# Strassen products in three of eight weight quads of a feed-forward's input pairs, on one core

## The chip, the cores and the metric

One core of a Trainium2 chip runs the whole program once. The metric is device time in microseconds (us), the median of three runs. The matrix engine is TensorE (PE); its products land in PSUM, eight banks of 512 float32 columns per partition. VectorE (DVE) and ScalarE (ACT) work element by element, SyncE (SP) issues the loads.

## The reference

A transformer layer of width 2048 for 256 tokens, in float32: a feed-forward, a mixer, a second feed-forward, a final norm.

```python
def swiglu(h, w_in, w_out):
    a, b = jnp.split(h @ w_in, 2, axis=-1)
    return (jax.nn.silu(a) * b) @ w_out
...
        x = x + 0.5 * swiglu(rmsnorm(x, ffn1_norm[l]), ffn1_w_in[l], ffn1_w_out[l])
        x = x + hybrid_mixer(rmsnorm(x, mix_norm[l]), ...)
        x = x + 0.5 * swiglu(rmsnorm(x, ffn2_norm[l]), ffn2_w_in[l], ffn2_w_out[l])
```

`w_in` is 2048 x 11264 (two halves of 5632 columns, for `a` and `b`), `w_out` 5632 x 2048. The mixer is one projection of 2048 x 13312, three branches (convolution, pooling, attention) with output products and gates, and a last product of 2048 x 2048. All that this change rewrites in substance is `h @ w_in` of the two feed-forwards.

## The kernel before, in words

Tokens lie in two tiles of 128. Every large product is cut into chunks of 512 output columns, each chunk into groups of four k-tiles of 128 rows. A group is one load of 1 MB (`raw`, 128 partitions x 4 x 512), from `emit_dma` (L106) on SP's queue, three buffers deep. To keep float32 accuracy on the faster product type, both operands are split into a high part, a rounded copy, and a low part, the rest. `emit_split` does that for half a group at a time: ACT copies 1024 columns (`whi`, L119), DVE subtracts (`wlo`, L120). `emit_mm` (L133) then issues three products for each k-tile and token tile: high x high, high x low, low x high; a product reads 512 columns and adds into a PSUM accumulator of two banks (`acc`, two buffers; `side` for transposes and the like, two buffers).

The order of the program is written out by the loop at the end (from L569): for each group and half group it issues the load three groups ahead, the split three half groups ahead, one pending side step (`pop_side`: transposes and small products that follow an evacuation by a few half groups), and the products. Each engine runs its own instructions in that order.

A feed-forward (`ffn`, L207) has eleven pairs of chunks. The pair's first chunk (`a`) is evacuated through ACT's sigmoid (L219) and a DVE product (L221), the second (`b`) multiplies into the same tile (L229); eight transposes (L174) turn the gated tile, and it is split into `gh`, `gl` (L157, L158). After six pairs, and again after the other five, four output chunks are multiplied and added to the residual `xr` (L244).

At the start the loads go out in quarters. The first two chunks take turns, so that x is needed more slowly; x comes in four quarters (`x0raw`), each scaled by the norm's gain and split on ACT (L165) and DVE (L166).

Of the kernel before, what the change touches and what calls it, by code (L numbers as in the profile page):

```python
# [26 lines left out]
FF_HALVES = (6, 5)  # L27
KH = 2
WHOLE = ((0, KH),)
HALVES = tuple((k, k + 1) for k in range(KH))  # L30
UNITS = 29
RAW_BUFS = 3
SPLIT_BUFS = 5
LOOK_DMA = 3
LOOK_SPLIT = 3
# [3 lines left out]
SQ = 13  # L39
# [18 lines left out]
def hybrid_trunk(ctx: ExitStack, tc: tile.TileContext, x, xT, wst, vecs, poolw, fnorm, consts, out):  # L58
# [4 lines left out]
    up = ctx.enter_context(tc.tile_pool(name="up", bufs=UNITS))  # L63
    wp = ctx.enter_context(tc.tile_pool(name="wp", bufs=RAW_BUFS))
    sp = ctx.enter_context(tc.tile_pool(name="sp", bufs=2))
    psA = ctx.enter_context(tc.tile_pool(name="psA", bufs=2, space=bass.MemoryType.PSUM))
    psB = ctx.enter_context(tc.tile_pool(name="psB", bufs=2, space=bass.MemoryType.PSUM))
# [4 lines left out]
    dist = cp.tile([P, P + S], F32, name="dist")  # L72
    pw = {}

    def unit(name, dt, shape=(P, KG, S)):
        """A tile of 4 KiB per partition; all of them share one set of buffers."""
        return up.tile(list(shape), dt, tag="unit", name=name)
# [6 lines left out]

    def side_psum():
        return psB.tile([P, KG, S], F32, tag="side", name="side")

    groups = []
# [3 lines left out]
    def chunk(lhs, nk, evac, tail=False):  # L92
        """One 512-column chunk of a product: lhs(i) gives the split transposed operand of k-group i."""
        ch = {}
        for i in range(nk):
            groups.append(dict(lhs=lhs, i=i, first=i == 0, last=i == nk - 1, evac=evac, tail=tail, chunk=ch))

    raw_t, split_t = {}, {}

    def emit_dma(n, cuts=1):  # L100
        if n >= len(groups):
            return
# [4 lines left out]

    def emit_split(m, parts=WHOLE):
        n, half = divmod(m, KG // KH)
        if n >= len(groups):  # L110
            return
        r = raw_t[n]
        if m not in split_t:
            split_t[m] = (wp.tile([P, KH, CH], F32R, tag="hi", name="whi", bufs=SPLIT_BUFS),
                          wp.tile([P, KH, CH], F32R, tag="lo", name="wlo", bufs=SPLIT_BUFS))
        h, l = split_t[m]
        for k0, k1 in parts:
            rv = r[:, half * KH + k0:half * KH + k1]
            nc.scalar.activation(h[:, k0:k1], rv, AF.Copy)  # L119
            nc.vector.tensor_sub(l[:, k0:k1], rv, f32(h[:, k0:k1]))  # L120

    def emit_mm(m, tt, acc, cols=slice(0, CH)):
        n, half = divmod(m, KG // KH)
        g = groups[n]
        h, l = split_t[m]
        ah, al = g["lhs"](g["i"])
        for k in range(KH):
            ka = half * KH + k
            todo = [(i, t, a, b) for t in tt for i, a, b in ((0, ah, h), (1, ah, l), (2, al, h))]
            if n == 0:  # L130
                todo.sort(key=lambda e: (0, 2, 1)[e[0]])
            for i, t, a, b in todo:
                nc.tensor.matmul(acc[t], a[:, ka, t * P:(t + 1) * P], b[:, k, cols],  # L133
                                 start=g["first"] and ka == 0 and i == 0,
                                 stop=g["last"] and ka == KG - 1 and i == 2)
# [3 lines left out]
    def later(*steps):  # L139
        """PE work that follows an evacuation: one step at a time, some half groups after it."""  # L140
        for i, f in enumerate(steps):
            urgent.append((now[0] + DELAY + i * GAP, f))
# [27 lines left out]
    def transpose8(src, ps):  # L170
        """src(t, k): [128 tokens, 128 channels]; ps[channel, k, token]."""
        for k in range(KG):
            for t in range(NT):
                nc.tensor.transpose(ps[:, k, t * P:(t + 1) * P], src(t, k), idn)  # L174
# [394 lines left out]
    for n in range(len(groups)):  # L569
# [11 lines left out]
        if n in (0, 2):  # L581
            load_xT(n // 2 + 2)
# [170 lines left out]
```

## Time and profile before

| | |
|---|---|
| median of three runs | 2297.21 us (2296.74 to 2297.72) |
| profiled execution, first to last instruction | 2295.9 us |
| PE busy | 2285.1 us |
| DVE busy | 1207.4 us |
| ACT busy | 1015.2 us |
| granted PE clock, mean | 0.999 |
| loads, mean over the span | 191 GB/s |

The median is 1.3 us above the profiled execution's span. Busy time of PE is modelled at the ends of its pipelined products, so a busy PE says only that it did not wait; the price of a product is read from long unbroken stretches. Idle time of DVE and ACT costs nothing as long as PE is not waiting for them.

### The profile page before, as it was taken

The numbers are of one execution on the slowest core, as the hardware profiler recorded it, in microseconds if no ns is written. First come the engines' busy times: TensorE is split into PE (matmuls) and PEld (weight loads), VectorE is DVE, ScalarE is ACT, GpSimd is POOL, SyncE is SP. The second block draws the span as 40 slices with busy tenths as digits, with TensorE's granted clock in tenths as the row PEclk, the third lists the DMA queues.
The fourth block names the chain that finished last, engine by engine and source line by source line (L and its number), as shares of the span: only waits on it lengthen the run. The fifth ranks groups of instructions, "written<-read, shape, count | busy, mean of one in ns | idle before, by whom it ended". The sixth has DMA issues, their size and how long they took to land.

```text
span 2295.9 us, 25201 instructions
## 1 busy us (share of the span) xinstructions
PE 2285.1 (100%) x10349; PEld 1895.8 (83%) x10349; DVE 1207.4 (53%) x1206; ACT 1015.2 (44%) x1140; POOL 3.7 (0%) x9
## 2 busy tenths in 40 slices
PE   9999999999999999999999999999999999999998
PEld 7888888888888888888888888888888888888887
DVE  6554544545555565544554554555554544545554
ACT  6444433434445444445554444354444433444443
POOL 0000000000000000000000000000000000000000
PEclk9999999999999999999999999999999999999999
DMA  8545555555445545454545555445555455545454
GB/s 317 186 189 193 186 185 205 194 183 197 177 179 216 194 166 202 181 192 172 188 165 184 207 196 184 183 184 186 199 181 204 183 183 203 199 185 185 183 201 147
DMA packets 63476, 438.68 MB, mean 191 GB/s; under 512 B 7168, under 2 KB 7936, under 8 KB 11264
## 3 DMA queue, kind: packets, MB, share of 16 engines
q1 hardware_dynamic: 63360, 437.06, 51.8%
q8 instruction: 81, 1.33, 0.2%
q14 instruction: 35, 0.29, 0.0%
HBM read 434.94 MB, written 2.10 MB: 190 GB/s over the span
## 4 chain that ended last, share of the span: by engine, by line
PE 99%; DMA 0%; SPq 0%; DVE 0%; issue 0%; POOLq 0%; ACT 0%; DVEq 0%
PE acc L133 94%; PE side L133 2%; PE side L174 2%; DMA raw<-w_dram 0%; PE side L449 0%; PE side L331 0%; PE side L359 0%; PE side L360 0%; PE side L330 0%; PE side L302 0%; PE side L301 0%; SPq L551 0%; SPq L552 0%; PE side L348 0%; PE side L349 0%; PE side L350 0%
## 5 line engine op out<-in xcount | busy, mean ns | idle before, releaser
L120 DVE TENSOR_TENSOR wlo<-raw,whi 128x1024 fp32r<-128x1024 f32 (+1 forms) x820 | 982.9, 1218 | 699.8 <-ACT whi L119 696.1
L119 ACT ACTIVATE whi<-raw 128x1024 fp32r<-128x1024 f32 (+1 forms) x820 | 851.1, 1055 | 840.2 <-PE acc L133 820.9
L133 PE MATMUL acc<-whi,x1h 128*128 128x512 f32 x832 | 327.7, 394 | 0.0
L133 PE MATMUL acc<-whi,x1l 128*128 128x512 f32 x832 | 324.1, 390 | 0.0
L133 PE MATMUL acc<-wlo,x1h 128*128 128x512 f32 x832 | 323.8, 389 | 0.0
L133 PE MATMUL acc<-whi,x2h 128*128 128x512 f32 x704 | 274.8, 390 | 0.0
L133 PE MATMUL acc<-whi,x2l 128*128 128x512 f32 x704 | 274.0, 389 | 0.0
L133 PE MATMUL acc<-wlo,x2h 128*128 128x512 f32 x704 | 273.9, 389 | 0.0
L133 PE MATMUL acc<-whi,gh 128*128 128x512 f32 x684 | 266.8, 390 | 0.0
L133 PE MATMUL acc<-wlo,gh 128*128 128x512 f32 x684 | 266.2, 389 | 0.0
L133 PE MATMUL acc<-whi,gl 128*128 128x512 f32 x684 | 266.2, 389 | 0.0
L133 PE MATMUL acc<-whi,x0h 128*128 128x512 f32 x640 | 249.8, 390 | 0.0
L133 PE MATMUL acc<-whi,x0l 128*128 128x512 f32 x640 | 249.1, 389 | 0.0
L133 PE MATMUL acc<-wlo,x0h 128*128 128x512 f32 x640 | 249.0, 389 | 0.0
L133 PEld LDWEIGHTS acc<-whi,x1l 128*128 128x128 f32 x832 | 156.2, 188 | 33.0
L133 PEld LDWEIGHTS acc<-whi,x1h 128*128 128x128 f32 x832 | 156.3, 188 | 31.5
L133 PEld LDWEIGHTS acc<-wlo,x1h 128*128 128x128 f32 x832 | 156.3, 188 | 31.3
L133 PEld LDWEIGHTS acc<-whi,x2l 128*128 128x128 f32 x704 | 132.1, 188 | 27.6
L133 PEld LDWEIGHTS acc<-wlo,x2h 128*128 128x128 f32 x704 | 132.2, 188 | 27.1
L133 PEld LDWEIGHTS acc<-whi,x2h 128*128 128x128 f32 x704 | 132.2, 188 | 27.1
L133 PEld LDWEIGHTS acc<-whi,gl 128*128 128x128 f32 x684 | 128.4, 188 | 26.9
L133 PEld LDWEIGHTS acc<-wlo,gh 128*128 128x128 f32 x684 | 128.4, 188 | 26.4
(167 smaller groups left out, 1790.9 us busy)
## 6 DMA issues: line engine op xcount, KB each, us to landing
raw<-w_dram SPq DMA_DIRECT2D x405, 1024.0 KB, 4.9
raw<-w_dram SPq DMA_DIRECT2D x8, 256.0 KB, 6.4
xr<-x_dram SPq DMA_DIRECT2D x2, 1024.0 KB, 9.9
out_dram<-xr SPq DMA_DIRECT2D x8, 256.0 KB, 2.8
x0raw<-xT_dram SPq DMA_DIRECT2D x3, 512.0 KB, 7.9
raw<-w_dram SPq DMA_DIRECT2D x2, 512.0 KB, 7.9
pw<-poolw_dram SPq DMA_DIRECT2D x2, 512.0 KB, 7.1
fn<-fnorm_dram SPq DMA_DIRECT2D x2, 512.0 KB, 6.8
```

What stands on the lines that cost most here:

```text
L119: nc.scalar.activation(h[:, k0:k1], rv, AF.Copy)
L120: nc.vector.tensor_sub(l[:, k0:k1], rv, f32(h[:, k0:k1]))
L133: nc.tensor.matmul(acc[t], a[:, ka, t * P:(t + 1) * P], b[:, k, cols], start=g["first"] and ka == 0 and i == 0, stop=g["last"] and ka == K ...
L174: nc.tensor.transpose(ps[:, k, t * P:(t + 1) * P], src(t, k), idn)
```

## The change

**Quads.** The pair's two chunks are now one set of four outputs (a and b, two token tiles each), made from eight quads of weights. A quad holds four blocks of 128 x 512: two k-tiles of the `a` columns (B11, B21) and the same two of the `b` columns (B12, B22). With two k-tiles of tokens (A11, A12 for tile 0, A21, A22 for tile 1) it is a product of 2 x 2 blocks. A plain quad ("P") takes eight block products. A summed quad ("S") takes seven, by Strassen's scheme in Winograd's form, from four sums of weight blocks, made in place in the raw buffer (`block_sums`, L238 to L241), and four sums of token blocks (`sum_forms`, made once). The pattern is `SPSPSPPP`; the first set of each feed-forward is plain. Each block product is still three instructions (high x high, high x low, low x high; L292).

**Banks.** PSUM is one tile of eight banks, placed by hand. In a set with sums all eight hold partial results. Banks K1, K6, K7, K5 are done after the last summed quad; three early steps (`e1` to `e3`, L422 to L430) combine them during the plain quads that follow. After the set four more additions (L438 to L441) finish a and b, then sigmoid (L446) and gate products (L449) as before. The eight transposes of the gated tile (L370) run two quads from the next set's end, in two halves, in banks K1 and K6.

**Ring.** High and low parts of weights live in two rings of 18 blocks of 512 columns, handed out block by block in the order in which they came free. `prepare` makes the parts of one step; `prepare_ahead` prepares as many steps ahead as blocks are free. A piece of several blocks is one instruction only where the blocks lie side by side. In the mixer eight blocks are lent to other tiles.

**Parts.** A feed-forward is in four parts of 3, 3, 2 and 3 sets, each followed by its share of the output product (four chunks of 3, 3, 2, 3 steps), so residual evacuations (now L493) double. The very last chunk has three groups; its second token tile is still made in two halves of 256 columns.

**Start.** The interleaving of the first two chunks is gone; the order of loads is nearly the same.

```diff
-FF_HALVES = (6, 5)
+PARTS = (3, 3, 2, 3)
+PATTERN = "SPSPSPPP"
+UNITS = 20
 RAW_BUFS = 3
-SPLIT_BUFS = 5
 LOOK_DMA = 3
-LOOK_SPLIT = 3
+RING = 18
+LEND = 10
...
+    def pair(forms, pattern, early, evac):
...
+            if kind == "S":
+                mm = [[("A", 1, A12, K2), ("T", 0, F5, K5), ("T", 3, F7, K7), ("T", 2, F6, K6)],
+                      [("T", 1, A22, K4), ("A", 2, F3, K3), ("A", 0, A11, K1)]]
+                if q == 0:
+                    mm = [mm[0][1:] + mm[1][2:], mm[0][:1] + mm[1][:2]]
+            else:
+                mm = [[("W", B11, A11, K2), ("W", B21, A12, K2), ("W", B11, A21, K4), ("W", B21, A22, K4)],
+                      [("W", B22, A12, K3), ("W", B12, A11, K3), ("W", B22, A22, K22), ("W", B12, A21, K22)]]
...
+    def ring(n, what, count):
+
+        got = [free.pop(0) for _ in range(count)]
...
+    def high(n, runs):
+        for i, b, c in runs:
+            nc.scalar.activation(whi[:, b:b + c], raw_t[n][:, i:i + c], AF.Copy)
+
+    def low(n, runs):
+        for i, b, c in runs:
+            nc.vector.tensor_sub(wlo[:, b:b + c], raw_t[n][:, i:i + c], f32(whi[:, b:b + c]))
+
+    def block_sums(n):
+
         r = raw_t[n]
...
+        nc.vector.tensor_add(r[:, 0], r[:, 0], r[:, 3])
+        nc.vector.tensor_add(r[:, 3], r[:, 3], r[:, 2])
+        nc.vector.tensor_add(r[:, 2], r[:, 2], r[:, 0])
+        nc.vector.tensor_add(r[:, 1], r[:, 1], r[:, 2])
...
+    def prepare(n):
+        a = first_of(n + 1)
+        ra = ring(n + 1, a, SIZE[a]) if a else ()
+        if steps[n]["kind"] == "S":
+            rt = ring(n, "T", 4)
+            high(n + 1, ra)
+            block_sums(n)
+            high(n, rt)
+            low(n + 1, ra)
+            low(n, rt)
+            emit_dma(n + LOOK_DMA)
+        else:
+            high(n + 1, ra)
+            low(n + 1, ra)
+        if a == "W":
+            emit_dma(n + 1 + LOOK_DMA)
+
+    def prepare_ahead():
+        while prepared[0] < len(steps) and need(prepared[0]) <= len(free):
+            prepare(prepared[0])
+            prepared[0] += 1
...
+        def e1():
+            t["pu"], t["vw"] = tok_tile("pu"), tok_tile("vw")
+            nc.scalar.activation(t["pu"][:, 0], pb(K1), AF.Copy)
+            nc.vector.tensor_sub(t["pu"][:, 1], t["pu"][:, 0], pb(K6))
+
+        def e2():
+            u = t["pu"][:, 1:2].to_broadcast((P, 2, CH))
+            nc.vector.tensor_add(t["vw"], bank[:, K7:K7 + 2], u)
+
+        def e3():
+            nc.vector.tensor_add(t["pu"][:, 1], t["vw"][:, 0], pb(K5))
...
+                nc.vector.tensor_add(a[0], pb(K2), a[0])
+                nc.vector.tensor_add(a[1], pb(K4), a[1])
+                nc.vector.tensor_sub(b[0], pb(K3), b[0])
+                nc.vector.tensor_sub(b[1], pb(K22), b[1])
...
+            nxt = steps[cur[0] + 1]["kind"]
+            if nxt == "C":
+                later(turn(0), turn(1), delay=4, gap=1)
+            else:
+                later(turn(0), turn(1), delay=1 + 2 * 6, gap=2)
...
-        for hf, cnt in enumerate(FF_HALVES):
+        for p, cnt in enumerate(PARTS):
...
+                in_set(n, xs, c, gs, first if c == 0 else PATTERN)
...
-    groups[:8] = [groups[4 * (i % 2) + i // 2] for i in range(8)]
...
+        if n in (0, 2, 4):
+            forms_xT(n // 2 + 1)
...
+        if n < tail_from:
+            prepare_ahead()
```

How the order moves on the engines, at three places. Names: `raw` the loaded weights, `whi`, `wlo` their parts, `bank` PSUM, `pu`, `vw` the partial sums in SBUF, `gt` the gated tile, `x0raw` the quarters of x, `fh`, `fhl` their parts (`x0h` before).

ACT at the start, from the first copy of x. Before:

```order
L165 ACTIVATE x0h<-x0raw,vec 128x256
L119 ACTIVATE whi<-raw 128x512
L165 ACTIVATE x0h<-x0raw,vec 128x256
L119 ACTIVATE whi<-raw 128x512
L165 ACTIVATE x0h<-x0raw,vec 128x256
L119 ACTIVATE whi<-raw 128x512
L165 ACTIVATE x0h<-x0raw,vec 128x256
L119 ACTIVATE whi<-raw 128x512 x5
L165 ACTIVATE x0h<-x0raw,vec 128x256 x4
L119 ACTIVATE whi<-raw 128x1024 x4
```

And now:

```order
L348 ACTIVATE fh<-x0raw,vec 128x256
L229 ACTIVATE whi<-raw 128x512
L348 ACTIVATE fh<-x0raw,vec 128x256
L229 ACTIVATE whi<-raw 128x512 x3
L348 ACTIVATE fhl<-x0raw,vec 128x256 x2
L348 ACTIVATE fh<-x0raw,vec 128x256 x2
L348 ACTIVATE fhl<-x0raw,vec 128x256 x2
L229 ACTIVATE whi<-raw 128x2048 x3
```

The four copies of the second quarter of x stood behind the copies of the second group's weights and now stand ahead of them, and those are one piece of 2048 columns.

DVE around a pair's third summed quad, up to the early evacuation L423. Before, half a pair with its evacuations:

```order
L229 SCALAR_TENSOR_TENSOR gt_931<-acc_942,rstd_501,gt_931 128x512 x2
L120 TENSOR_TENSOR wlo_1078<-raw_1005,whi_1077 128x1024
L120 TENSOR_TENSOR wlo_1095<-raw_1039,whi_1094 128x1024
L120 TENSOR_TENSOR wlo_1113<-raw_1039,whi_1112 128x1024
L158 TENSOR_TENSOR gl_1126<-side_1116,gh_1125 128x1024
L120 TENSOR_TENSOR wlo_1142<-raw_1075,whi_1141 128x1024
L120 TENSOR_TENSOR wlo_1160<-raw_1075,whi_1159 128x1024
L120 TENSOR_TENSOR wlo_1176<-raw_1110,whi_1175 128x1024
L120 TENSOR_TENSOR wlo_1194<-raw_1110,whi_1193 128x1024
L120 TENSOR_TENSOR wlo_1210<-raw_1157,whi_1209 128x1024
L221 SCALAR_TENSOR_TENSOR gt_1225<-acc_1081,rstd_501,gt_1225 128x512 x2
```

And now, in the second set of the first feed-forward's fourth part:

```order
L233 TENSOR_TENSOR wlo_77<-raw_3966,whi_76 128x512
L238 TENSOR_TENSOR raw_3966<-raw_3966 128x512
L239 TENSOR_TENSOR raw_3966<-raw_3966 128x512
L240 TENSOR_TENSOR raw_3966<-raw_3966 128x512
L241 TENSOR_TENSOR raw_3966<-raw_3966 128x512
L233 TENSOR_TENSOR wlo_77<-raw_4050,whi_76 128x512 x4
L233 TENSOR_TENSOR wlo_77<-raw_3966,whi_76 128x512 x4
L233 TENSOR_TENSOR wlo_77<-raw_4052,whi_76 128x512 x4
L233 TENSOR_TENSOR wlo_77<-raw_4123,whi_76 128x512 x4
L233 TENSOR_TENSOR wlo_77<-raw_4125,whi_76 128x512 x3
L423 TENSOR_TENSOR pu_4198<-pu_4198,bank_78 128x512
L427 TENSOR_TENSOR vw_4199<-bank_78,pu_4198 128x1024
```

Block sums and the early evacuation have come in, and the low parts are mostly in pieces of 512 columns.

ACT ahead of the early evacuation `e1` (L422) of the same set, of the change alone:

```order
L229 ACTIVATE whi_76<-raw_3884 128x512 x4
L229 ACTIVATE whi_76<-raw_3966 128x1024
L229 ACTIVATE whi_76<-raw_3966 128x512
L229 ACTIVATE whi_76<-raw_4050 128x512 x4
L229 ACTIVATE whi_76<-raw_3966 128x512 x4
L229 ACTIVATE whi_76<-raw_4052 128x512 x4
L229 ACTIVATE whi_76<-raw_4123 128x512 x4
L229 ACTIVATE whi_76<-raw_4125 128x512 x3
L422 ACTIVATE pu_4198<-bank_78 128x512
L467 ACTIVATE gh_4228<-bank_78 128x512
```

The copy out of bank K1 stands behind the copies of the third quad's sums, of the three plain quads and of the next set's first three blocks, which are the last row ahead of it.

## Rows read from the trace of the kernel before

**Rows 1.** The page: span, busy time (part 1) and slices (part 2).

```profile
span 2295.9 us, 25201 instructions
...
PE 2285.1 (100%) x10349; PEld 1895.8 (83%) x10349; DVE 1207.4 (53%) x1206; ACT 1015.2 (44%) x1140; POOL 3.7 (0%) x9
...
PE   9999999999999999999999999999999999999998
...
PEclk9999999999999999999999999999999999999999
```

**Rows 2.** Chain of waits in time: start us, us, what.

```profile
11.49 39.95 PE side L133 x174
...
235.44 43.54 PE acc L133 x192
...
279.85 174.11 PE acc L133 x768
...
2280.86 7.20 PE side L133 x60
```

**Rows 3.** PE waits: engine line, releaser, us in total, times, longest.

```profile
PE side L133 <- ACT whi L119: 1.6, 2, 0.8
```

**Rows 4.** DVE by line and form: xcount | busy us, mean ns.

```profile
L120 DVE TENSOR_TENSOR wlo<-raw,whi 128x1024 fp32r<-128x1024 f32 x812 | 977.5, 1223 | 696.4 <-ACT whi L119 692.6
L229 DVE SCALAR_TENSOR_TENSOR gt<-acc,rstd,gt 128x512 f32<-128x512 f32 x42 | 29.6, 747 | 65.6 <-PE acc L133 65.6
...
L120 DVE TENSOR_TENSOR wlo<-raw,whi 128x512 fp32r<-128x512 f32 x8 | 5.4, 692 | 3.4 <-ACT whi L119 3.4
```

**Rows 5.** DVE timeline, first input sets: start us, us, instructions.

```profile
164.27 1.41 DVE L221 SCALAR_TENSOR_TENSOR gt<-acc,rstd,gt 128x512 f32<-128x512 f32 x2 [4.42 <-ACT gt L219]
165.60 3.48 DVE L120 TENSOR_TENSOR wlo<-raw,whi 128x1024 fp32r<-128x1024 f32 x3
```

**Rows 6.** DVE timeline, end, two dependent operations.

```profile
2280.89 0.69 DVE L638 SCALAR_TENSOR_TENSOR xr<-acc,xr 128x512 f32<-128x512 f32 x1 [4.00 <-PE acc L133]
2281.62 0.69 DVE L640 SCALAR_TENSOR_TENSOR junk<-xr 128x512 f32<-128x512 f32 x1
```

**Rows 7.** Tile raw, last line: all its loads.

```profile
DMA to landing us min/median/max: 3.3/4.9/11.0
```

**Rows 8.** Windows at the start: PE, PEld, DVE, ACT, POOL, clock, DMA, GB/s.

```profile
6.00:10.00 4.00, 3.86 (x16) 2.65 (x15) 2.92 (x6) 2.47 (x5) 0.00 (x0) 1.00 0.82 264
10.00:14.00 4.00, 3.19 (x14) 2.27 (x14) 2.69 (x5) 3.07 (x5) 0.00 (x0) 1.00 0.97 352
14.00:18.00 4.00, 4.00 (x20) 3.30 (x19) 3.06 (x7) 3.34 (x7) 0.00 (x0) 1.00 1.03 427
```

**Rows 9.** ACT by line and form: weight copies.

```profile
L119 ACT ACTIVATE whi<-raw 128x1024 fp32r<-128x1024 f32 x812 | 846.1, 1059 | 837.2 <-PE acc L133 820.9 <-PE side L133 10.0 <-DMA raw<-w_dram 3.4
...
L119 ACT ACTIVATE whi<-raw 128x512 fp32r<-128x512 f32 x8 | 5.1, 632 | 3.0 <-DMA raw<-w_dram 2.9
```

**Rows 10.** SP's waits: the weight load's.

```profile
SPq L106 <- DVE wlo L120: 2047.2, 401, 10.4
```

**Rows 11.** ACT timeline at the start.

```profile
10.80 3.29 ACT L119 ACTIVATE whi<-raw 128x512 fp32r<-128x512 f32 x5 [1.16 <-DMA raw<-w_dram]
14.76 1.71 ACT L165 ACTIVATE x0h<-x0raw,vec 128x256 fp32r<-128x256 f32 x4 [0.66 <-DMA x0raw<-xT_dram]
```

**Rows 12.** PE timeline at the start: products after a wait.

```profile
5.66 0.73 PE L133 MATMUL side<-whi,x0h 128*128 128x512 f32 x2 [0.82 <-ACT whi L119]
...
6.70 0.62 PE L133 MATMUL side<-wlo,x0h 128*128 128x512 f32 x2
```

**Rows 13.** PE by line and form: the warm-up products.

```profile
L536 PE MATMUL side<-warm 128*128 128x512 bf16 x9 | 3.7, 585 | 1.2 <-DVE mhalf L531 1.2
```

More of the change, by code (lines that the diff above doesn't have):

```diff
@@ L83, in tok_tile, with take, wide @@
         return unit(name, dt, (P, NT, CH))
-    def side_psum():
-        return psB.tile([P, KG, S], F32, tag="side", name="side")
-    groups = []
+    turn_of = {}
+    def take(*starts):
+        i = turn_of.get(starts, 0)
+        turn_of[starts] = i + 1
+        return starts[i % len(starts)]
+    def wide(b):
+        return bank[:, b:b + 2].rearrange("p b (k s) -> p (b k) s", s=S)
+    def side_psum():
+        at = steps[cur[0]]
+        if at["kind"] != "C":
+            assert not at["set"]["sums"]
+            return wide(K6)
+        return wide(take(4, 6) if at["far"] else 6)
@@ L89, in hybrid_trunk, with side_bank, chunk @@
+    def side_bank():
+        at = steps[cur[0]]
+        b = take(6, 7) if at["kind"] == "C" else take(K1, K6)
+        return bank[:, b].rearrange("p (k s) -> p k s", s=S)
+    steps = []
+    cur = [0]
     urgent = deque()
     lazy = deque()
-    def chunk(lhs, nk, evac, tail=False):
+    def chunk(lhs, nk, evac, at=(0, 2), far=True, tail=False):
         ch = {}
         for i in range(nk):
-            groups.append(dict(lhs=lhs, i=i, first=i == 0, last=i == nk - 1, evac=evac, tail=tail, chunk=ch))
@@ L100, in emit_dma @@
+    raw_t, parts_t = {}, {}
+    free = list(range(RING))
     def emit_dma(n, cuts=1):
-        if n >= len(groups):
+        if n >= len(steps) or n in raw_t:
             return
@@ L122, in emit_mm @@
[L122 to L125, printed above, removed]
-        ah, al = g["lhs"](g["i"])
[L127 to L135, printed above, removed]
+    def ring(n, what, count):
+        got = [free.pop(0) for _ in range(count)]
+        parts_t[n, what] = got
+        runs = []
+        for i, b in enumerate(got):
+            if runs and runs[-1][1] + runs[-1][2] == b:
+                runs[-1][2] += 1
+            else:
+                runs.append([i, b, 1])
+        return runs
@@ new lines, in emit_mm @@
+    def emit_mm(n, ks, tt, acc, cols=slice(0, CH)):
+        g = steps[n]
+        ah, al = g["lhs"](g["i"])
+        for k in ks:
+            b = parts_t[n, "W"][k]
+            for t in tt:
+                ts = slice(t * P, (t + 1) * P)
+                for i, (a, w) in enumerate(three(ah[:, k, ts], al[:, k, ts], b)):
+                    nc.tensor.matmul(acc[t], a, w[:, cols], start=g["first"] and k == 0 and i == 0,
+                                     stop=g["last"] and k == KG - 1 and i == 2)
@@ L137, in hybrid_trunk, with later @@
     now = [0]
[L139 to L142 removed]
+    def later(*todo, delay=None, gap=None):
+        for i, f in enumerate(todo):
+            urgent.append((now[0] + (delay or DELAY) + i * (gap or GAP), f))
     def pop_side(force=False):
@@ L568, in hybrid_trunk @@
     tail = []
-    for n in range(len(groups)):
-        g = groups[n]
+    tail_from = len(steps) - PARTS[-1]
+    for n, g in enumerate(steps):
+        cur[0] = n
         if n == n_ffn1 - 2:
@@ L651, in hybrid_trunk @@
     for t, c0, c1, o in tail:
-        for m in range(end, len(groups) * PER):
-            emit_mm(m, (t,), {t: o}, slice(c0, c1))
+        for n in range(tail_from, len(steps)):
+            emit_mm(n, range(KG), (t,), {t: o}, slice(c0, c1))
         finish(t, c0, c1, o, 2 + (c0 > 0))
```

399 lines of the change are left out of this document (283 added, 116 removed).

## The prediction

> **What bounds the kernel now.** I read the page first. TensorE (PE) is busy over the whole span, in all 40 slices and at full clock, while VectorE (DVE) is busy for 53% of it and ScalarE (ACT) for 44% [rows 1]. The chain of waits then gives the price of one product. The reader should see long unbroken stretches: 768 products of 512 columns in 174.11 us, 0.2267 us each, and 0.87 us for the eight transposes between two stretches (279.85 - 235.44 - 43.54) [rows 2]. PE's table of waits holds hardly more than 1.6 us, at the start [rows 3]. So time is the number of products by 0.2267 us; the helpers are free as long as PE never waits. The question is whether they stay free. The span is 2295.9 us [rows 1], 1.3 below the median of the runs, 2297.2; I take that 1.3 as what lies around a span, and sum against the median.
>
> **Products removed.** A summed quad has seven products where a plain one has eight, each in three parts: 21 instructions for 24. Three such quads a pair, ten pairs in each feed-forward (the first one stays plain): 2 x 10 x 9 = 180 fewer, 40.8 us. The last output chunk shrinks from five groups to three, so 48 of its products of 256 columns become 24 of 512; sixty of 256 columns take 7.20 us, 0.12 each [rows 2], so 48 x 0.12 - 24 x 0.2267 = 0.3 us. Together **-41.1**, all on PE's path: 2256.1 if PE never waits. The transposes stay as many.
>
> **What DVE must do for one pair.** One VectorE operation on 512 columns lasts 692 ns, one on 1024 lasts 1223 [rows 4], so each further block of 512 in a piece costs 0.53. Independent operations overlap: two of 747 ns take 1.41 us, the second starting 0.084 before the first ends, and three of 1223 ns take 3.48 [rows 5]. So a piece of 512 costs 0.61. Dependent ones don't: 0.73 from start to start for 692 ns [rows 6]. The row listing of the change has, in the pair whose last rows are quoted (from one L423 to the next), 39 pieces for 41 ring blocks, since the ring hands out scattered blocks: 39 x 0.607 + 2 x 0.53 = 24.7. Block sums, a chain of four for each of three quads: 12 x 0.73 = 8.8. Combining the banks: L423, L427 and L430 2.7, the four additions L438 to L441 2.4, the four gate products L449 2.7, the two splits L468 1.2. Sum **42.5 us**. PE needs 183 x 0.2267 + 0.87 = 42.4 for the same pair, where it needed 44.4. DVE had 47% spare; in these pairs it has none.
>
> **What the loads add to that.** A raw buffer of a summed quad is free only when its last low part is made, and the load three steps on goes out then. In the kernel before, SP too waited for DVE's low parts (2047 us in 401 waits) [rows 10], without harm, since a buffer came free every 5.4 us. A load lands 4.9 us after its issue [rows 7]; the next one, issued with it, a transfer later (1 MB at 427 GB/s, 2.5 us [rows 8]). Then ACT copies a block (0.63 [rows 9]) and DVE makes the low parts of the plain quad and of the sums, eight blocks: 4.9 + 0.6 + 8 x 0.61 + 0.1 = 10.5 us from issue to issue. PE needs 45 x 0.2267 = 10.2 for that quad pair. In the 5.5 us ahead of the first low part DVE has the four block sums, 2.9, and then idles 2.6. In the first of the three rounds the additions and gate products of the pair before fill that; in the other two they don't: 5.2 us. Of L423 to L430 (2.7), which follow the third round, I count half as falling into it, 1.3. So preparing a pair takes 42.5 + 5.2 - 1.3 = 46.4 us, **4.0 us longer than PE needs**. The ends: 0.1 (every idle filled) and 5.3 (none).
>
> **Where that reaches PE.** The ring holds prepared blocks, but queues are in order. The copy L422, which empties bank K1, stands on ACT behind the copies of everything prepared ahead, the next pair's first blocks included (the listing). PE needs K1 for transposes one plain quad later, 24 x 0.2267 = 5.4 us. So helpers may be 5.4 us behind at that point and no more, however full the ring is. Each part's output product lets them catch up: there a step takes PE 5.4 us and DVE some 4 x 0.61. Within a part the lag grows by 4.0 a pair: none is lost in the first summed pair, 8.0 - 5.4 = 2.6 by the second, 12.0 - 5.4 = 6.6 by the third. The two feed-forwards have four parts with two summed pairs and four with three: 4 x 2.6 + 4 x 6.6 = **+36.8**.
>
> **The start.** In the kernel before, 174 of the first 192 products run from 11.49 us on [rows 2], so the first group ends at 11.49 + 6 x 0.2267 = 12.9. ACT had copied the second group by 14.1, block by block, and only then the second quarter of x, which landed at 14.76 [rows 11]. Now these four copies of x come first, until 16.5, then one copy of 2048 columns (0.63 + 3 x 0.43 = 1.9), until 18.4, then one low part of 2048 (0.69 + 3 x 0.53 = 2.3), until 20.7. PE's second product of that step needs it: 20.7 - 12.9 = 7.8. Between 5, if that quarter lands sooner, and 8 I take **+7.5**.
>
> **Small terms.** In a part of two pairs, PE has one step (5.4 us) between the last pair's end and its gated product; additions, gate products, transposes and split take 2.4 + 2.7 + 0.4 + 1.8 = 7.3: 2 us, twice, **+4**. After a wait two products take 0.73 where two take 0.62 else [rows 12]: 0.11 for some 40 waits, **+4**. The 32 added output evacuations on DVE (0.69 each) and the shorter ring in the mixer I cost at nothing: DVE's half-empty steps cover them; without that cover, 22 us and some 5. Loads keep their bytes.
>
> **Sum.** 2297.2 - 41.1 + 36.8 + 7.5 + 4 + 4 = **2308**, 0.5% slower.
>
> [...] Rows 5 show independent operations starting 0.084 us early. [...]
>
> **Rivals.**
> *The idle time is filled* (the other side). If DVE runs its sums and bank work inside the load waits, the lag per pair d falls. The waits are 4(2d - 5.4) + 4(3d - 5.4), each bracket not below zero: nothing at d under 1.8, 21 at 3.2, 30 at 3.7. With start and small terms this gives 2264 to 2272 without waits, and up to 2293 at d = 3.2, the point from which it decides. For it: only 0.8 us more work a pair falling into the idles does it. Against: DVE's own work already equals PE's.
> *A wash*, d between 3.2 and 3.7: 2293 to 2302.
> *No idle filled*, d = 5.3: 4 x 5.2 + 4 x 10.5 = 62.8, so 2334. For it: all these operations wait on one landing.
> *The clock drops* at the 12 waiting pairs. Nine warm-up products of the same 512 columns took 3.7 us, 0.41 each [rows 13]; if 24 products ran at that, 24 x 0.18 x 12 = 53 more, 2361. Against: rows 8.
> *No overlap on DVE*, 49 independent operations a pair at 0.085 more: d = 8.2, waits 4 x 11 + 4 x 19.2 = 121, 2392. Against: rows 5.
> That the products aren't removed is excluded by the listing: 9576 products of 512 columns for 9732.
>
> **How the numbers follow.** A measurement tells 0.2% (4.6 us) from nothing: faster is under 2292.6, slower over 2301.8. The forecast (d from 3.7 to 5) gets 0.42, no idle filled 0.12, the clock 0.04, no overlap 0.02: slower 0.60. The wash 0.14. The filled idle 0.26, faster. The range runs from 2276 (d = 2.2: 2297.2 - 41.1 + 15.5 + 4.8) to 2334; outside lie some 0.12 below and 0.07 above. The likeliest case alone spans 2302 to 2328.
>
> **What would show it.** PE's products of the input sets fall to 183 a pair. PE's waits, nearly none now, rise to some 50 us, led by DVE's low parts (L233) and ACT's copy L422. First summed pairs of a part take about 42.4 us, third ones 46 to 49. DVE is busy for over 90% inside third pairs, and SP's load waits end with low parts there. A start wait of 5 to 8 us stands at the second step. I am wrong if third pairs run at 42 to 43 us (then 2265 to 2275), if the waits sit in output products, or if the granted clock leaves 1.00.

## The result, and the profile after

| | before | after |
|---|---|---|
| median of four runs | 2297.22 us (2296.74 to 2297.72) | 2329.3 us (2328.35 to 2331.18) |
| profiled span | 2295.9 us | 2327.4 us |
| PE busy, DVE busy | 2285.1, 1207.4 us | 2302.2, 1623.2 us |

The changed kernel is slower: ratio 1.0141, 95% interval [1.0126, 1.0155], 32 us. The forecast was 11 us slower; the sign is right and the time lies in the range, but the terms that made the sum are wrong in both directions, as the runs below show.

The page of the changed kernel: span, busy time, and DVE by slices. To compare with [rows 1].

```profile
span 2327.4 us, 27342 instructions
...
PE 2302.2 (99%) x10145; PEld 1864.4 (80%) x10145; DVE 1623.2 (70%) x2482; ACT 1189.3 (51%) x2012; POOL 4.2 (0%) x9
...
DVE  6986896877975666544654545556886896877984
```

PE has 204 fewer instructions (10145 for 10349 in [rows 1]), the sums do what they say, and DVE went from 53% to 70% busy. Yet PE is *busy* for 17 us more than before. Fewer products and more busy time: a product must have become dearer. The chain of waits in time (start us, us, what) shows it.

```profile
20.33 73.32 PE bank L292 x302
...
161.50 55.99 PE bank L303 x240
217.48 74.20 PE bank L292 x318
...
347.73 8.40 PE bank L303 x36
```

The run of 318 products of the input sets takes 74.20 us, 0.2333 each, and 240 output products 55.99, 0.2333 each. Before, 768 took 174.11, 0.2267 each [rows 2]. These runs have no wait in them. The three sets of that part lie between 217.48 and 347.73: 130.3 us, of which 549 products at 0.2333 are 128.1 and two times eight transposes 1.7. So hardly 0.5 us of waits is left where the prediction had 6.6 for a part of three pairs. PE's table of waits (engine line, releaser, us in total, times, longest) agrees:

```profile
PE bank L292 <- ACT whi L229: 6.4, 2, 5.2
PE bank L303 <- DVE gl L468: 2.6, 2, 1.3
PE bank L292 <- DVE wlo L233: 2.6, 6, 1.5
PE bank L303 <- ACT whi L229: 2.4, 1, 2.4
...
PE bank L303 <- DVE wlo L233: 0.8, 1, 0.8
```

Low parts for input sets (L233), which were to lead the table with most of 37 us, have 2.6, and 1.8 of that belongs to the start.

In the mixer the two prices stand side by side. PE's timeline there (start us, us, the instruction, what it writes and the tiles that it reads):

```profile
1229.05 0.39 PE L303 MATMUL bank<-wlo,whi 128*128 128x512 f32 x1
...
1235.85 0.39 PE L303 MATMUL bank<-wlo,whi 128*128 128x512 f32 x1
...
1236.31 0.39 PE L303 MATMUL bank<-whi,x1h 128*128 128x512 f32 x1
...
1241.91 0.39 PE L303 MATMUL bank<-whi 128*128 128x512 f32 x1
```

In the mixer some token tiles lie in blocks lent by the two rings, and the trace then names them `whi` or `wlo`. From 1229.05 to 1235.85 all are of that sort: 30 products in 6.80 us, 0.2267 each. The 24 from 1236.31 to 1241.91 have `x1h` and `x1l`, which lie in tiles of their own: 5.60 us, 0.2333 each. So it is throughout: 0.227 for the 2256 products whose tokens lie in a ring (three groups of 752 on the page), 0.2333 for the other 7320 of 9576. The second group costs 7320 x 0.0066 = 48 us more than it would at the old price.

What differs between them is where the two operands of a product stand in SBUF. In the kernel before, a tile of 8 bytes (`mhalf`) stands ahead of the token tiles and takes 32 (it is laid at byte 35264 of a partition, the first token tile at 35296); tokens, raw buffers and weight parts all follow it in blocks of 4096 and 8192 bytes, so that every operand stands at the same place modulo 2048 (all at 480). In the changed kernel the rings come first (35264 and 72128), then `mhalf` (108992), then the token tiles (from 109024): tokens stand 32 bytes further than weights.

### The profile page after: what moved, and what is told of

Read it like the earlier page. It is cut to its first block, busy times and chain, and to the rows that moved or that the text cites. A ratio compares the mean times of both kernels' runs of the same rounds, so it can differ in the third digit from the quotient of the medians.

```text
span 2327.4 us, 27342 instructions
## 1 busy us (share of the span) xinstructions
PE 2302.2 (99%) x10145; PEld 1864.4 (80%) x10145; DVE 1623.2 (70%) x2482; ACT 1189.3 (51%) x2012; POOL 4.2 (0%) x9
## 4 chain that ended last, share of the span: by engine, by line
PE 92%; DVE 5%; issue 1%; DMA 1%; ACT 1%; SPq 0%; POOLq 0%; DVEq 0%; ACTq 0%
PE bank L303 54%; PE bank L292 35%; DVE wlo L233 3%; PE bank L370 1%; DVE gt L449 1%; DVE gl L468 0%; DMA pw<-poolw_dram 0%; DMA x0raw<-xT_dram 0%; DVE raw L239 0%; DVE raw L240 0%; ACT whi L229 0%; DVE raw L238 0%; PE bank L716 0%; DVE pu L441 0%; PE bank L617 0%
## 5 line engine op out<-in xcount | busy, mean ns | idle before, releaser
L233 DVE TENSOR_TENSOR wlo<-raw,whi 128x512 fp32r<-128x512 f32 (+3 forms) x1638 | 1111.8, 741 | 338.4 <-ACT whi L229 336.6
L229 ACT ACTIVATE whi<-raw 128x512 fp32r<-128x512 f32 (+3 forms) x1638 | 1003.8, 669 | 621.4 <-PE bank L303 258.7
L292 PE MATMUL bank<-whi,fhl 128*128 128x512 f32 x1760 | 573.0, 398 | 5.2 <-ACT whi L229 5.2
L292 PEld LDWEIGHTS bank<-whi,fhl 128*128 128x128 f32 x1760 | 332.0, 189 | 84.7 <-ACT whi L229 5.7
L292 PE MATMUL bank<-wlo,fhl 128*128 128x512 f32 x880 | 349.2, 397 | 1.5 <-DVE wlo L233 1.5
L303 PE MATMUL bank<-whi 128*128 128x512 f32 x752 | 297.2, 395 | 2.4 <-ACT whi L229 2.4
L303 PE MATMUL bank<-wlo,whi 128*128 128x512 f32 x752 | 293.4, 390 | 0.8 <-DVE wlo L233 0.8
L303 PE MATMUL bank<-whi,wlo 128*128 128x512 f32 x752 | 294.0, 391 | 0.0
L303 PE MATMUL bank<-whi,gl 128*128 128x512 f32 (+1 forms) x684 | 268.6, 393 | 2.6 <-DVE gl L468 2.6
L303 PE MATMUL bank<-whi,gh 128*128 128x512 f32 (+1 forms) x684 | 269.8, 394 | 0.5 <-ACT gh L467 0.5
L292 PEld LDWEIGHTS bank<-wlo,fhl 128*128 128x128 f32 x880 | 166.1, 189 | 40.8 <-DVE wlo L233 2.0
L292 PE MATMUL bank<-wlo,fh 128*128 128x512 f32 x468 | 185.9, 397 | 1.2 <-DVE wlo L233 1.0
L292 PE MATMUL bank<-whi,fh 128*128 128x512 f32 x468 | 185.3, 396 | 1.2 <-ACT whi L229 1.2
L292 PE MATMUL bank<-whi,fl 128*128 128x512 f32 x468 | 185.1, 395 | 0.0
L493 DVE SCALAR_TENSOR_TENSOR xr<-bank,xr 128x512 f32<-128x512 f32 x62 | 42.8, 691 | 135.7 <-PE bank L303 135.4
```

What stands on the lines that cost most here:

```text
L229: nc.scalar.activation(whi[:, b:b + c], raw_t[n][:, i:i + c], AF.Copy)
L233: nc.vector.tensor_sub(wlo[:, b:b + c], raw_t[n][:, i:i + c], f32(whi[:, b:b + c]))
L292: nc.tensor.matmul(bank[:, k], a, b, start=e["start"][at + j] and i == 0, stop=e["stop"][at + j] and i == 2)
L303: nc.tensor.matmul(acc[t], a, w[:, cols], start=g["first"] and k == 0 and i == 0, stop=g["last"] and k == KG - 1 and i == 2)
L493: nc.vector.scalar_tensor_tensor(xv, acc[:, t], 0.5, xv, op0=ALU.mult, op1=ALU.add)
```

## Experiments

### Is it the place?

Four kernels move tiles by 32 or 64 bytes. The first two are the changed kernel with a larger `mhalf`, in the second with 32 bytes ahead of the rings too; the other two are the kernel before with its weights moved, alone or together with its tokens.

```diff
-    mhalf = cp.tile([P, NT], F32, name="mhalf")
+    mhalf = cp.tile([P, 16], F32, name="mhalf")
```

The second has this as well:

```diff
+    pad = cp.tile([P, 8], F32, name="pad")
     whi = cp.tile([P, RING, CH], F32R, name="whi")
```

The kernel before gets 32 bytes in the pool of its raw buffers, which moves these and the weight parts; the last kernel has the larger `mhalf` too, which moves the tokens and, by 32 more, brings the weights back to 32 past a multiple of 64. So in both the weights stand 32 bytes further than the tokens, at two different places:

```diff
+    pad = wp.tile([P, 8], F32, tag="pad", name="pad", bufs=1)
```

> The changed kernel with the tiles of tokens (the stationary operands) moved up by 32 bytes per partition, nothing else. In the changed kernel the two rings of weights begin at a multiple of 64 bytes, the token tiles 32 bytes past one; in the kernel before both stood 32 bytes past one. Theory (the two operands' places differ by 32 bytes, and that costs 6.6 ns a product): products at 0.2267 us everywhere, 7329 x 0.0066 = 48 us less PE time, of which waits for DVE give some back, since PE gets 1.2 us faster a pair: 2285 to 2300 us. Rival (the pitch comes from the order of banks, of operands or of the ring): products stay at 0.2333, 2329 us.

> The changed kernel with rings and token tiles both 32 bytes past a multiple of 64, as in the kernel before. Theory (only the difference counts): as the run with both at a multiple, 0.2267 us a product, 2285 to 2300 us. Rival (operands 32 bytes past a multiple are slow in themselves): all products at 0.2333 or slower, those of the mixer with ring tiles too: 2329 to 2345 us.

> The kernel before with raw buffers and weight tiles moved up by 32 bytes, so that weights stand at a multiple of 64 and token tiles 32 past one, as in the changed kernel. Theory: all 9732 products at 0.2333, 9732 x 0.0066 = 64 us more: 2361 us. Rival (the pitch belongs to the changed program): 2297 us.

> The kernel before with only the token tiles moved up by 32 bytes: tokens at a multiple of 64, weights 32 past one. Theory (the difference counts, in either direction): 2361 us. Rival (what costs is a moving operand at a multiple of 64 with a stationary one beside it): 2297 us.

Measured: 2328.96 us (ratio to the kernel before 1.0141 [1.0124, 1.0158]) and 2328.65 (1.0138 [1.0123, 1.0153]), both as the changed kernel; 2359.36 (1.0269 [1.0254, 1.0284]) and 2359.58 (1.0270 [1.0254, 1.0285]), both 62 us slower than the kernel before. The chain of the kernel before with its weights moved has

```profile
1230.11 179.20 PE acc L135 x768
```

which is 0.2333 a product for the stretch that took 174.11 in [rows 2]; the other one has the same 179.20. So a shift of 32 bytes between the operands makes the dearer product, in a program that is otherwise untouched and at either of two places: the rival (the pitch, from one product's start to the next one's, belongs to the changed program) is out. Here the weights stand further, in the changed kernel the tokens do. The last kernel was to move the tokens alone; it moves the weights as well, and keeps the difference of the one before it. The first two were misses. They put both operands at a multiple of 64, or both 32 past one, but 64 bytes apart in terms of 2048; agreement modulo 64 isn't enough.

### How far must they agree?

The next kernel takes `mhalf` from a pool that lies behind the token tiles, so that tokens begin a multiple of 2048 bytes from the rings. One with padding between its 20 token tiles, and letters in their names, maps the distance; one has no sums.

```diff
-    mhalf = cp.tile([P, NT], F32, name="mhalf")
+    mhalf = sp.tile([P, NT], F32, tag="mhalf", name="mhalf", bufs=1)
```

The map has, beside this, so many bytes ahead of each token tile:

```diff
+    gaps = [0, 32, 32, 64, 128, 128, 128, 256, 256, 256, 256, 256, 224, 32, 0, 0, 0, 0, 0, 0]
```

The one without sums has, beside the first edit:

```diff
-PATTERN = "SPSPSPPP"
+PATTERN = "PPPPPPPP"
```

> The changed kernel with its small tile mhalf taken from behind the token tiles, so that these begin a multiple of 2048 bytes from the rings (in the kernel before, all operands stand at the same place modulo 2048; the shift of 32 bytes cost 62 us there, and in the changed kernel a shift to a difference of 64 bytes gained nothing). Theory (the operands' places must agree modulo more than 64 bytes): 0.2267 us for all products, 48.6 us less of PE time; PE then is 1.2 us faster a pair, and waits for DVE come back, 4 x 0.8 + 4 x 3.9 less the 2 there are, 17 us: 2298, between 2281 (no wait comes back) and 2299. Rival (what is slow is the place of the token tiles as such): 2329.

> The same kernel with the token tiles at differences of 0, 32, 64, 128, 256, 384, 512, 768, 1024, 1280, 1536, 1792 and 2016 bytes (modulo 2048) from the rings and the last seven at 0 again, and names that tell the tile, so that one trace shows the pitch of a product for each difference. Theory: 0.2267 at 0 and from some power of two on at its multiples, 0.2333 at the others; 32, 64 and 2016 are slow by the runs so far. The rival has 0.2333 at all of them, 0 included.

> The changed kernel with agreeing places and no sums: all sets plain, so that ring, banks, four parts and the start stand alone. Eight blocks for seven: 180 products more, 40.8 us. DVE has 24 fewer operations a pair and no chain on a raw buffer, so that no pair waits. Theory: the kernel before plus start (7.6), its slow products (3.3), the mixer's entry (6.2) and the two part turns (6): about 2320, at least 2305. If the ring and the parts cost nothing it is 2297.

With agreeing places: **2288.85 us**, ratio 0.9961 [0.9947, 0.9975] to the kernel before; 2298 was expected, with 17 us of the 48 coming back as waits; some 8 came back, 6.7 of them in PE's tables of waits (16.5 us in the changed kernel, 23.2 here). The same change, with one tile of 8 bytes elsewhere, is faster than the kernel before by 8.9 us and faster than the changed kernel by 40.4. Its chain:

```profile
160.14 54.45 PE bank L303 x240
214.59 72.10 PE bank L292 x318
...
342.00 8.16 PE bank L303 x36
...
1204.01 174.11 PE bank L303 x768
```

318 products take 72.10 where they took 74.20, and 768 take 174.11, the very number of [rows 2].

The map (a single run, 2306.3 us). Its timeline at the first products of three steps of 24, `i` at a distance of 1024 bytes, `a` at 0 and `d` at 128, and of the step behind them:

```profile
1993.01 0.40 PE L298 MATMUL bank<-whi,fhl_i 128*128 128x512 f32 x1
...
1998.48 0.39 PE L298 MATMUL bank<-whi,fhl_a 128*128 128x512 f32 x1
...
2003.93 0.40 PE L298 MATMUL bank<-whi,fhl_d 128*128 128x512 f32 x1
...
2009.52 0.39 PE L298 MATMUL bank<-whi,fh_j 128*128 128x512 f32 x1
```

5.47, 5.45 and 5.59 us. The mean from start to start over all products whose own token tile and the next one's stand at the same distance from the ring:

| distance modulo 2048 | products | ns |
|---|---|---|
| 0; tokens in a ring | 2205; 2147 | 227; 227 |
| 256, 512, 768 | 239, 103, 59 | 228, 229, 227 |
| 1024, 1280, 1536, 1792 | 509, 140, 78, 74 | 226, 228, 227, 227 |
| 32, 64, 128 | 328, 277, 246 | 232, 235, 233 |
| 384, 2016 | 95, 345 | 234, 232 |

Starts are given to 10 ns, hence the scatter. At a multiple of 256 bytes the product is cheap, elsewhere it is dear. "From some power of two on, at its multiples" held; the power is 256, as far as these thirteen distances tell. Inside a tile the slices that products read begin at multiples of 512 bytes, so that modulo 512 they are seven: 0 and 256 are cheap, the other five dear.

Without sums, with agreeing places: 2324.1 us, ratio 1.0114 [1.0099, 1.0129]. The ring, the four parts and the new start cost 26.4 us by themselves, more than the 23 expected. By the starts of PE's products, and against the kernel before, some 9.3 of them lie at the start, 8.4 at the mixer's entry, 2.0 in its branches, 3.0 from its last product to the second feed-forward's first step, and 1.9 at the turns of the short parts: 24.6, an estimate from the two traces. The largest of its waits:

```profile
PE bank L292 <- ACT whi L229: 7.1, 2, 5.9
PE bank L303 <- ACT whi L229: 4.2, 1, 4.2
```

Both waits of the first row are at the start; the second row is the mixer's entry, where ACT stands at the copy of the pooling weights until their load lands. The products behind the start's waits are slow, as in the changed kernel (below): over the first 62 us the granted clock is 0.92 on average in both, for 1.00 in the kernel before.

Put in a row, the runs divide the way from the kernel before to the changed one: 2297.7 (before) + 26.4 (everything but the sums) - 35.3 (the sums, 2288.85 - 2324.13) + 40.4 (the places) = 2329.2. Each term is the difference of two runs that follow each other, so the row ends at the changed kernel's 2329.3 whatever they are: that it closes shows nothing. What the sums are worth with the dearer product was not run.

### Waits at the start and at the mixer, and DVE's reserve

All three have the agreeing places. The first takes both waits away; `split_early(m, c)` makes high and low parts of step m in pieces of c blocks:

```diff
+        if n == 0:
+            split_early(1, 1)
         if n in (0, 2, 4):
             forms_xT(n // 2 + 1)
+        if n == 0:
+            split_early(2, 2)
...
         if n == n_ffn1 - 2:
...
-                nc.scalar.activation(pw[c][0], raw, AF.Copy)
-                nc.vector.tensor_sub(pw[c][1], raw, f32(pw[c][0]))
...
+        if n == n_ffn1 + 1:
...
+                nc.scalar.activation(pw[c][0], raw, AF.Copy)
+                nc.vector.tensor_sub(pw[c][1], raw, f32(pw[c][0]))
```

The second gives DVE more to do, in `block_sums`:

```diff
         nc.vector.tensor_add(r[:, 1], r[:, 1], r[:, 2])
+        nc.vector.tensor_copy(extra, r[:, 1])
```

The third is the first with all four sums moved like this one:

```diff
-        nc.vector.tensor_add(r[:, 0], r[:, 0], r[:, 3])
+        nc.gpsimd.tensor_add(r[:, 0], r[:, 0], r[:, 3])
```

> The changed kernel with agreeing places, and two waits taken away: at the start the weights of the second and third step are split in pieces and ahead of the next quarter of x; at the mixer's entry the copies of the pooling weights stand three steps after their loads instead of right behind them. In the run with agreeing places (2288.9) the start lost 8.4 us in waits and some 3 in slower products, the entry 4.6 and 3. Theory (these are PE's own losses): 8 and 7 us less, 2274, within 2270 to 2281. Rival (PE only gets ahead of DVE and waits for it later): 2282 or more.

> The changed kernel with agreeing places (2288.9) and one more DVE copy of 512 columns behind each quad's block sums, three a pair, some 0.6 us each: 1.9 us a pair. It tells how far DVE is from the bound. DVE's period in a pair was 43.6 us there for PE's 42.4, so the lag grows from 1.2 to 3.1 a pair. Theory with the tolerance that the waits there show (third pairs wait 0.75, so 3 x 1.2 - 0.75 = 2.8): third pairs lose 6.5, second ones of parts with two 3.4, together 40 for some 6 now: 2322. The prediction's tolerance of 5.4: 4 x 0.8 + 4 x 3.9 = 19: 2302. Rival (DVE has reserve that its load waits hide): under 2293.

> The run with both waits taken away, and the four block sums of a quad on GpSimd instead of DVE: DVE has 8.8 us less to do a pair. Theory (the waits for low parts in third pairs come from DVE's load alone): they vanish, 7 us less than that run, about 2267. Rival (GpSimd's sums are slow, or slow DVE down beside them; no row shows one): the chain of four comes late and PE waits in every summed quad, 2290 or far more.

*Both waits taken away:* 2285.22 us, ratio 0.9946 [0.9932, 0.9961]; 3.6 less for 15 expected. The entry's wait is gone from PE's table, and by the starts of PE's products some 7 us come back there, as expected. The start's wait is not gone, it moved:

```profile
PE bank L292 <- ACT whi L229: 8.1, 2, 6.9
PE bank L292 <- DVE wlo L233: 6.6, 8, 1.7
```

The 6.9 now stands at 58.8 us, ahead of the first summed quad. PE gets through the first pair sooner and then waits for block sums and copies that stand behind the squares of x and the sums of its blocks on ACT and DVE. The rival was right for the start. Some 1.6 us more are lost behind one turn of a short part, where the granted clock fell to 0.50 in this run (from 501.2 us on).

*More load:* 2302.93 us, ratio 1.0023 [1.0014, 1.0033]; 14 us more than without. The copy takes 0.43 and adds 0.47 to DVE's queue, 1.4 us a pair, less than the 1.9 assumed. In PE's table:

```profile
PE bank L294 <- DVE wlo L234: 17.6, 23, 2.1
```

17.6 us in 23 waits where the kernel without the copies has 7.2 in 10 (below). DVE has little reserve: of 20 pairs x 1.4 = 28 us, half reaches PE. Neither model of the tolerance fits: with a lag of 1.2 + 1.4 = 2.6 a pair the prediction's gives 4 x 2.4, less the 6 already there, 2293, so that 2302 is met in number only; the other gives 4 x 5.0 + 4 x 2.4 less 6, 2313. The waits are short ones at L292, spread over second and third pairs, and none is for L422's copy.

*Sums on GpSimd:* 2283.62 us, ratio 0.9939 [0.9924, 0.9954]; 1.6 less for 7. A sum takes two to three times as long there (means of 1.48 to 1.89 us, where DVE's are 0.68 to 0.69 with agreeing places), and DVE's work beside it gets slower too. The groups by line and shape (names, shapes, count | busy us, mean ns | idle before):

```profile
L238 POOL TENSOR_TENSOR raw<-raw 128x512 f32<-128x512 f32 x60 | 113.2, 1887 | 808.2 <-DVE wlo L233 808.2
...
L240 POOL TENSOR_TENSOR raw<-raw 128x512 f32<-128x512 f32 x60 | 88.7, 1479 | 5.3 <-DVE wlo L233 0.7
```

```profile
L233 DVE TENSOR_TENSOR wlo<-raw,whi 128x512 fp32r<-128x512 f32 x1508 | 1059.7, 762 | 281.8 <-ACT whi L229 279.5
...
L449 DVE SCALAR_TENSOR_TENSOR gt<-pu,rstd,gt 128x512 f32<-128x512 f32 x40 | 34.3, 857 | 0.0
...
L468 DVE TENSOR_TENSOR gl<-bank,gh 128x512 fp32r<-128x512 f32 x42 | 28.6, 684 | 7.1 <-ACT gh L467 6.4
```

The first two groups in the same kernel with the sums on DVE (*both waits taken away*):

```profile
L233 DVE TENSOR_TENSOR wlo<-raw,whi 128x512 fp32r<-128x512 f32 x1508 | 943.2, 685 | 274.0 <-ACT whi L229 271.5
...
L449 DVE SCALAR_TENSOR_TENSOR gt<-pu,rstd,gt 128x512 f32<-128x512 f32 x40 | 29.7, 743 | 0.0
```

So DVE's low part of 512 columns takes 762 ns for 685, the gate product 857 for 743. These are averages over all; by the times in the trace, 224 low parts that lie wholly within a GpSimd sum take 1022 ns on average (675 to 1789), and the 1175 that touch none take 684. The waits of third pairs are mostly gone; the first summed pair, whose chain of sums is now longer, waits 7.6 us at its start.

### A version that beats both

Both start from the run with both waits taken away. `late_sums(q)` makes the sums of token blocks of quad q:

```diff
-        if 5 <= n < 8:
-            for q in range(8)[n - 5::3]:
...
+        if n == 5:
+            late_sums(0)
...
             prepare_ahead()
+        if n in (8, 9):
+            late_sums(2 * n - 14)
```

The second has this too, for all four sums:

```diff
+        eng = nc.gpsimd if n > 16 else nc.vector
-        nc.vector.tensor_add(r[:, 0], r[:, 0], r[:, 3])
+        eng.tensor_add(r[:, 0], r[:, 0], r[:, 3])
```

> The run with both waits taken away (2285.2), and two of the three sums of token blocks made a step after they were (behind the weights' parts of the first summed pair, not ahead). There the wait of the start had come back at the first summed quad, 7.1 + 2.2 us and slower products behind it, since ACT made the squares and all three sums first. Theory (it is the order of ACT's and DVE's queues): some 8 to 11 us less, 2275, within 2273 to 2279. Rival (the first set is bound by loads and helpers as a whole): the wait comes back further on, 2282 or more.

> The same, with the block sums of all but each program's first summed pair on GpSimd, where a sum takes 1.5 to 1.9 us for DVE's 0.69 and slows DVE's gate products beside it (0.86 for 0.75 us). In the run that had all of them there, third pairs no longer waited but for two. Theory (DVE's load makes third pairs' waits): 5 us less than the run beside it. Rival (the chain on GpSimd is late in its turn): the same time or more.

2282.23 us, ratio 0.9935 [0.9918, 0.9951]: 3 less for 8 to 11, again nearer the rival. The first pair's wait shrank, and waits for low parts rose a little (8.9 us in 12 for 6.6 in 8). With the sums on GpSimd from the second pair on: **2277.17 us**, ratio 0.9911 [0.9896, 0.9925], 5 less, as expected; 20.5 us faster than the kernel before and 52 faster than the changed one. What it still waits for:

```profile
PE bank L293 <- DVE wlo L233: 4.2, 5, 2.0
PE bank L304 <- DVE gl L469: 3.0, 2, 1.5
PE bank L293 <- ACT whi L229: 2.1, 2, 1.2
```

## Why the prediction was right and wrong

**Right sign, wrong terms.** The prediction had 11.5 for start and turns, nothing for the sums as a whole (-41.1 + 36.8 + 4 for restarts), and nothing for the rest. The runs give 26.4, -35.3 and 40.4. Errors of +15, -35 and +40 cancelled to 21. The right sign is luck: at 0.2267 us a product, the price that the prediction used, the change measures 2288.85, faster than the kernel before.

**The price of a product.** The step that failed first is "So time is the number of products by 0.2267 us": the price was taken for a constant of the product, and the sum carried 0.2267 from [rows 2] into a program whose tiles lie elsewhere. Here it is 0.2333 for 7320 of 9576 products, and an edit of one line takes it back, 40.4 us. In PE time it is 48; of the rest, some 8, PE's tables show 6.7 as waits that the slower product had hidden. None of the rivals has this, although the change moves every operand. The price was one of the few things that the prediction never put to doubt.

**What DVE costs.** "4.0 us longer than PE needs" a pair, hence **+36.8**, is the second. DVE's timeline with agreeing places, from the additions of one summed pair (L438) to those of the next, and on to the last of the part:

```profile
254.77 0.68 DVE L438 TENSOR_TENSOR pu<-bank,pu 128x512 f32<-128x512 f32 x1
...
262.59 6.57 DVE L233 TENSOR_TENSOR wlo<-raw,whi 128x512 fp32r<-128x512 f32 x9
269.08 0.68 DVE L238 TENSOR_TENSOR raw<-raw 128x512 f32<-128x512 f32 x1
...
271.86 7.24 DVE L233 TENSOR_TENSOR wlo<-raw,whi 128x1024 fp32r<-128x1024 f32 x11
280.33 2.43 DVE L233 TENSOR_TENSOR wlo<-raw,whi 128x1024 fp32r<-128x1024 f32 x3 [1.23 <-ACT whi L229]
282.94 0.69 DVE L233 TENSOR_TENSOR wlo<-raw,whi 128x512 fp32r<-128x512 f32 x1 [0.19 <-ACT whi L229]
283.89 1.23 DVE L233 TENSOR_TENSOR wlo<-raw,whi 128x1024 fp32r<-128x1024 f32 x1 [0.26 <-ACT whi L229]
...
298.41 0.68 DVE L438 TENSOR_TENSOR pu<-bank,pu 128x512 f32<-128x512 f32 x1
...
338.42 0.68 DVE L438 TENSOR_TENSOR pu<-bank,pu 128x512 f32<-128x512 f32 x1
```

From 254.77 to 298.41 are 43.6 us, where the prediction has 46.4. Its work is 43.6 - 1.7 = 41.9, close to the 42.5 worked out. The price of its pieces was right too: eleven low parts in 7.24 us, one of them of two blocks, where 11 x 0.607 + 0.53 is 7.2. But of the idle time, 5.2 - 1.3 = 3.9, there is 1.7: at 269.08 the second quad's sums follow the first one's low parts at once, its weights having landed, and only the third round waits, for ACT's copies (1.23, 0.19 and 0.26), of which the first and the last had waited for a load. And from the second pair's additions to the third's are 40.0 us, under PE's 42.4, since towards the part's end DVE prepares groups of the output product, which have no sums: two rounds of block sums lie in that stretch, three in the one before. So the lag grows by 1.2 once in a part of three pairs, not by 4.0 a pair. In time, the 180 products that the sums save are 40.8 us, and the run without sums is 35.3 slower: the sums cost 5.5 us net in waits and restarts, where the prediction has 36.8 + 4. What is left of the waits:

```profile
PE bank L292 <- ACT whi L229: 7.3, 2, 6.1
PE bank L292 <- DVE wlo L233: 7.2, 10, 1.5
```

7.2 us, 1.8 of them at the start. The rival *idle time is filled* gave d under 1.8 and no waits, 2264 to 2272 without the dearer product and the entry; its mechanism is what the trace shows, though its time is not. Third pairs, and one second pair, do wait, by 0.7 to 0.8 us, but at low parts (L233), while the place forecast, L422 and bank K1, has 0.2 us in one run and nothing in the others. Why waits start at a lag this small wasn't tried apart; the copy run shows only that 1.4 us more a pair costs 14.

**The start.** Forecast **+7.5** with the second product of the second step at 20.7 us: it starts at 20.33 us (the chain above), behind the low part that was named:

```profile
17.99 2.30 DVE wlo L233
```

Right, by the steps given. What was missing is the clock behind it. **Small terms:** two turns of short parts wait 1.3 us each in the changed kernel, for 2. The mixer's entry, 3.2 us of waits, is a term left out: the prediction costed the shorter ring there at nothing, and didn't look at the copy that waits for its own load. By the estimate from the run without sums, the start holds 9.3 of the 26.4, for 7.5 and some restarts, the turns 1.9 for 4, and 13.4 lie where the prediction put nothing: at the entry, in the mixer's branches and on the way to the second feed-forward.

**The clock.** The windows of the changed kernel: PE, PEld, DVE, ACT and POOL busy, then the granted clock, DMA share and GB/s.

```profile
12.40:20.30 7.90, 1.17 (x3) 0.29 (x1) 3.99 (x6) 5.85 (x7) 0.00 (x0) 0.72 1.03 422
20.40:26.40 6.00, 6.00 (x15) 4.70 (x16) 4.28 (x2) 1.80 (x2) 0.00 (x0) 0.53 1.01 395
```

Behind the start's wait, in which PE had three products in 7.9 us, the clock is 0.53 for 6 us. It falls to 0.52 behind the mixer's entry, in which PE had seven products in 5.1 us, and to 0.57 behind one of the two turns, and stays at 1.00 behind the other:

```profile
511.00:515.00 4.00, 4.00 (x18) 3.24 (x19) 0.37 (x1) 1.16 (x2) 0.00 (x0) 1.00 0.87 358
744.50:749.60 5.10, 1.88 (x7) 1.05 (x6) 4.14 (x5) 4.38 (x7) 0.00 (x0) 1.00 0.31 125
749.60:752.60 3.00, 3.00 (x9) 2.30 (x8) 1.99 (x5) 1.27 (x4) 0.00 (x0) 0.52 0.31 93
2076.00:2080.00 4.00, 2.53 (x14) 1.62 (x13) 4.00 (x7) 2.12 (x4) 0.00 (x0) 1.00 0.51 139
2080.40:2084.20 3.80, 3.80 (x11) 3.00 (x10) 0.24 (x1) 0.66 (x2) 0.00 (x0) 0.57 0.87 362
```

This is the clock rival, which had 0.04: not at the twelve places it named, but at three others. In the first stretch a product starts 0.43 us after the last, 0.2 more than the 0.2333 of the long runs (11 products from 20.92 to 25.62 us); PE worked 6.00, 3.00 and 3.80 us in the three stretches, which at that price loses some 6 us, an estimate (12.8 x 0.2 / 0.43). Ahead of the first two stretches PE was busy for 1.17 of 7.9 and 1.88 of 5.1 us, ahead of the third for 2.53 of 4 us; but ahead of the turn behind which the clock stayed it was busy for hardly less, 2.46 of the 4 us from 506.8. So what makes the clock fall these windows don't tell. The waits in third pairs show no such fall (0.15 to 0.3 us here, with the clock at 1.00 in the window of one, below; 0.7 to 0.8 with agreeing places, where the 83 products behind one take 19.11 us, 0.23 each), nor does the wait of 1.3 us at 509 us, behind which the first of these rows has 1.00. Away from the start, the clock fell inside a summed pair, the kind of place that the rival named, in the run with DVE's added copies: behind a wait of 2.1 us the window from 120.4 to 123.7 us has 0.50.

**What would have shown it.** PE's products fell to 183 a pair, as said; DVE's share in third pairs rose to about nine tenths, 38.63 us of 43.43 in the window of one (columns as above):

```profile
304.30:347.73 43.43, 43.28 (x190) 34.66 (x189) 38.63 (x58) 26.20 (x44) 0.00 (x0) 1.00 0.61 228
```

The start's wait is where it was put. "I am wrong if third pairs run at 42 to 43 us": at 43.4 here they lie just above, and in terms of 0.2267 they run at 42.4 and a wait of 0.7 to 0.8.

## What to carry to other kernels

A constant read from a trace is a constant of that program. When a change moves tiles, ask of every duration in the sum whether it could depend on where its operands lie, and first compare the price of the commonest instruction in the new trace with the old before any wait is looked for. Here a product cost 0.2267 us with its stationary and moving operands a multiple of 256 bytes apart and 0.2333 at the other distances tried, and one small tile allocated elsewhere was worth 40.4 us; so look at that distance when the price has changed. When a forecast comes out near the result, still check its terms: here three errors of 15 to 40 us summed to 21.

## What the runs showed of the hardware that was not expected

A product of 128 x 128 by 128 x 512 in `float32r` starts 0.2267 us after the last when both operands stand at the same place modulo 256 bytes of their partitions, and 0.2333 when they don't (768 in 174.11 or 179.20 us), at the thirteen distances of the map. Which of the two stands further doesn't matter (232 ns at distances 32 and 2016), and it shows as busy time of PE (2302.2 us for 2285.1, with fewer products), not as a wait. So the price depends on how the two operands lie to each other. What in the chip makes it so no run here shows.

With the block sums on GpSimd, DVE's operations beside them got longer: a low part that lies wholly within one takes 1022 ns on average, one that touches none 684. The low part of the gated tile, which reads PSUM and one operand in SBUF, isn't lengthened (L468: 22 of its 42 lie wholly within a GpSimd sum, at 675 to 693 ns; 677 to 693 in the same kernel with its sums on DVE). Why the one is lengthened and the other not was not tried apart.
